# Values of the differential attention computed two heads at a time, with 512 columns moving

## The chip, the cores and the metric

One NeuronCore of one Trainium2 chip runs the program. The metric is device time in microseconds (us) of one execution. TensorE (PE) multiplies matrices, PEld is its loading of the stationary operand, VectorE (DVE) and ScalarE (ACT) work element by element, GpSimd (POOL) and SyncE (SP) here mostly issue transfers. Each engine works through its own queue of instructions in order and waits on semaphores for the others.

## The reference, cut to what matters

A decoder trunk of two layers on 512 tokens of width 1024, in float32. Layer 0 mixes tokens by pooling, layer 1 by differential attention over a shared K/V; each layer also attends to 256 memory tokens and ends in a SwiGLU. What the change touches is the product that gives the shared values, and the product that uses them:

```python
kv = rmsnorm(h, g_kv) @ w_kv
k = kv[..., :DIFF_HEADS * 2 * DIFF_HD].reshape(b, s, DIFF_HEADS, 2, DIFF_HD)
v = kv[..., DIFF_HEADS * 2 * DIFF_HD:].reshape(b, s, DIFF_HEADS, DIFF_VD)
...
sc = jnp.einsum('bqhcd,bkhcd->bhcqk', qi, k).astype(jnp.float32) * scale
p = jax.nn.softmax(sc, axis=-1)
a = p[:, :, 0] - lam * p[:, :, 1]
return jnp.einsum('bhqk,bkhe->bqhe', a.astype(v.dtype), v)
```

There are 4 heads, and a head's values are 256 columns wide.

## The kernel before, in words

Every product is made in three: each operand is split into a high part and a low rest (`split`: ScalarE writes `hi`, a rounded copy, VectorE writes `lo`, source minus `hi`), and TensorE adds hi·hi, hi·lo and lo·hi into one bank of PSUM (`three`, `group`). So each weight tile of 512 KB is loaded by a DMA on SP into `raw` (line 198), cast by ScalarE to `whi` (line 177), and subtracted by VectorE to `wlo` (line 178). The pools for `raw`, `whi` and `wlo` have three buffers each.

The weight tiles stand in one list, `plan`, in the order of use. `weights()` hands out the next tile and calls `load_to`, which writes down the transfer and the split of the tiles up to two further on (`AHEAD`). So the two tiles that come next have their splits written into the queues while the present one is multiplied.

The second layer's attention part is a list of units, `SECOND`. A letter is a kind of unit, a figure which one: `Q` and `K` queries and keys of a differential head (PSUM tiles `qk`, 48 matmuls), `V` its values (tiles `v`), `q`, `k`, `v` the same of the memory attention, `h` an output tile of the memory attention (tiles `wo`, 24 matmuls), `a` and `b` the output of the differential attention for heads 0, 1 and 2, 3. Between the pieces of these units the planner `Pace` puts the matmuls of chains that run along: for the differential attention of head n, scores of 128 queries at a time (`dsc`, two products and a bfloat16 mask for each), transposes of the probabilities (`dtr`), the product with the values (`do`, after the event `dv`), and the norm of the result (`ps_st`, `ps_row`). ScalarE makes the exponentials `dp` and the splits `ath` of the transposes, VectorE the maxima `dmx`, the differences `dp` and the rests `atl`.

`diff_values(n)` of before is a call of `token_major`: for one head, the tokens are stationary in tiles of 128, and the weights of the head move, 256 columns at a time. One PSUM bank takes two token tiles, and all 8 blocks of the contraction are done for a token tile before the next one begins. Its two weight tiles hold 4 blocks of 256 columns each. When a bank is done, `leave` reads it in two halves, each with a `split` that multiplies by the tokens' scale `rc1` (ScalarE line 180, VectorE line 181).

The PSUM pool of these tiles (`ps_mm`) has four banks. TensorE's instructions are always kept in the program's order. Those of ScalarE and VectorE may be put in another order by the scheduler that builds the program; `queued` binds a split to the program's order while `first_loads[0]` is true, which in before it is only during the first loads of the kernel.

Of the kernel before, what the change touches and what calls it, by code (L numbers as in the profile page):

```python
# [16 lines left out]
P = 128  # L17
# [4 lines left out]
KD = D // P  # L22
KF = DFF // P
NT = S // P
# [12 lines left out]
AHEAD = 2  # L37
# [20 lines left out]
       (((0, 1), "", "sync"), ((4,), "pool", "sync"), ((2, 3), "", "scalar"), ((6,), "", "scalar"), ((7,), "", "sync"),  # L58
        ((5,), "pool", "scalar")))
R_C = 6.2  # L60
SECOND = "Q0 k0 q0 k1 v0 q1* v1 Q1 k2 q2* Q2 k3 Q3 q3* v2 v3 K0 h0 h1 h2 V0 h3 h4 K1 V1 h5 K2 V2 K3 a0 a1 a2 V3 a3 h6 h7 b0 b2 b1 b3"
WARM = (256, 256, 256, 256)
FIRST = "q0 q1 k0 i0 i2 i1 o0 k1* v0 o1 v1 i3 o2 k2 q2* o3 k3 v2 q3* v3"
PARTS = 2
# [41 lines left out]
def trunk(ctx, tc, xT, memT, w_in, w_out, w_out1, w_gate, w_up, w_down, w_mk, w_mv, pool_w, w_k, w_v,  # L106
          gains, lams, c_ident, c_mask, c_rope, c_cnt, out):
    nc = tc.nc
    V, A = nc.vector, nc.scalar
    pace = Pace()  # L110
    first_loads = [True]
# [11 lines left out]
    def slot(name, shape=(2, S), dtype=F32R, parts=P):  # L123

        return slots.tile([parts, *shape], dtype, tag="s", name=name)
# [7 lines left out]
    def duo(name):  # L133

        t = slot(name)
        return t[:, 0, :], t[:, 1, :]
# [4 lines left out]
    def mmps(name="mm"):  # L141
        return ps_mm.tile([P, S], F32, tag="mm", name=name)
# [10 lines left out]
    def mm(ps, l, r, start, stop, **more):  # L153
        tc.keep_in_program_order(nc.tensor.matmul(ps, lhsT=l, rhs=r, start=start, stop=stop, **more))  # L154
# [4 lines left out]
    def group(ps, terms, first=True, last=True, **more):  # L159
        n = len(terms)  # L160
        for i, (l, r) in enumerate(terms):
            mm(ps, l, r, first and i == 0, last and i == n - 1, **more)
            if i % 6 == 5 or i == n - 1:
                yield "pe", (i % 6 + 1) * r.shape[-1] / 2370

    def three(whi, wlo, xhi, xlo):
        return [(whi, xhi), (whi, xlo), (wlo, xhi)]

    def queued(ins):

        if first_loads[0]:
            tc.keep_in_program_order(ins)

    def split(src, hi, lo, scale=None):

        if scale is None:
            queued(A.copy(out=hi, in_=src))  # L177
            queued(V.tensor_tensor(out=lo, in0=src, in1=f(hi), op=ALU.subtract))  # L178
        else:
            queued(A.activation(out=hi, in_=src, func=AF.Copy, scale=scale))  # L180
            queued(V.scalar_tensor_tensor(out=lo, in0=src, scalar=scale, in1=f(hi), op0=ALU.mult, op1=ALU.subtract))


    class Load:
# [7 lines left out]
        def tiles(self):  # L192
            self.raw = raw_tile(self.kt, self.cols)
            self.hi, self.lo = cut_tiles(self.kt, self.cols)

        def part(self, ks):
            raw, hi, lo = [t[:, ks, :] for t in (self.raw, self.hi, self.lo)]
            nc.sync.dma_start(out=raw, in_=self.src[:, ks, :])
            split(raw, hi, lo)

        def fetch(self):
# [7 lines left out]
    plan, loaded, used, fetched = [], [], [0], [0]  # L209

    def load_to(n):
        while len(loaded) < min(n, len(plan)):
            i = len(loaded)
            while fetched[0] < len(plan) and fetched[0] <= i + plan[fetched[0]].early:
                plan[fetched[0]].fetch()
                fetched[0] += 1
            loaded.append(plan[i].parts())

    def weights():

        used[0] += 1
        load_to(used[0] + (AHEAD if isinstance(plan[min(used[0], len(plan) - 1)], Load) else AHEAD7))
        return loaded[used[0] - 1]

    def unit(loads, go, need=None):
        plan.extend(x if hasattr(x, "parts") else Load(*x) for x in loads)
        return go, need
# [14 lines left out]
    h = [res.tile([P, S], F32, tag=f"h{k}", name=f"h{k}") for k in range(KD)]  # L242
# [165 lines left out]
    def tile_of(src, kt=KD):  # L408
        return [(src[:, ks:min(ks + KD, kt), :], min(KD, kt - ks), P) for ks in range(0, kt, KD)]

    def proj(ps, xs, kt=KD):

        for ks in range(0, kt, KD):
            n = min(KD, kt - ks)
            whi, wlo = weights()
            terms = []
            for k in range(n):
                terms += three(whi[:, k, :], wlo[:, k, :], xs[0][ks + k], xs[1][ks + k])
            yield from group(ps, terms, ks == 0, ks + n == kt)
# [5 lines left out]
    mo = {0: [], 1: []}  # L425
# [32 lines left out]
    def token_major(src, xs, nt, cols, store, event, after):  # L458


        def go():
            w = [weights() for _ in range(2)]
            x, out = xs(), []
            for t2 in range(nt // 2):
                ps = mmps("v")
                a, b = duo("v")
                for m in range(2):
                    t = 2 * t2 + m
                    tk = slice(t * P, (t + 1) * P)
                    o = slice(m * 256, (m + 1) * 256)  # L470
                    terms = []
                    for k in range(KD):
                        whi, wlo = w[k // 4]
                        terms += three(x[0][k][:, tk], x[1][k][:, tk], whi[:, k % 4, :], wlo[:, k % 4, :])
                    yield from group(ps[:, o], terms)
                out.append((a, b))
                yield "spawn", leave(ps, t2, out)

        def leave(ps, t2, out):
            yield "need", after  # L480
            a, b = out[t2]
            for m in range(2):
                t = 2 * t2 + m
                o = slice(m * 256, (m + 1) * 256)
                split(ps[:, o], a[:, o], b[:, o], cols[:, t:t + 1])
            if t2 == nt // 2 - 1:
                store[event[1:]] = out
                pace.at(event, 2.0)

        return unit([(src[c], 4, 256) for c in range(2)], go)  # L490
# [83 lines left out]
    def out_tile(src, j, tiles, need=None, after=None):  # L574


        def go():
            t = tiles()
            ps = mmps("wo")
            yield from proj(ps, ([a for a, _ in t], [b for _, b in t]))  # L580
            V.tensor_tensor(out=h[j], in0=ps, in1=h[j], op=ALU.add)
            if after is not None:
                after(j)

        return unit(tile_of(src[j]), go, need)

    def out_pair(src, jj, tiles, need=None, after=None):


        def go():  # L590
            t = tiles()
            whi, wlo = weights()
            for i in range(2):
                j = 2 * jj + i
                ps = mmps("wo")
                sl = slice(i * P, (i + 1) * P)
                terms = []
                for k in range(4):
                    terms += three(whi[:, k, sl], wlo[:, k, sl], *t[k])
                yield from group(ps, terms)  # L600
                V.tensor_tensor(out=h[j], in0=ps, in1=h[j], op=ALU.add)
                if after is not None:
                    after(j)

        return unit([(src[jj], 4, 256)], go, need)
# [255 lines left out]
    diff_q, diff_k, diff_v = {}, {}, {}  # L861
# [30 lines left out]
    def diff_qk(src, n, xs, store, event, rb=None, need=None):  # L892
        def go():
            pss = []
            for c in range(2):
                ps = mmps("qk")
                yield from proj(ps, xs())
                pss.append(ps)
            store[n] = roped(pss, rb)
            pace.at((event, n), R_ROPE)  # L900

        return unit(tile_of(src[2 * n]) + tile_of(src[2 * n + 1]), go, need)

    def diff_values(n):
        return token_major(w_v[n], lambda: xk, NT, rc1, diff_v, ("dv", n), "rb1")

    def diff_scores(n, probs, s0):
        yield "need", ("dk", n)
# [88 lines left out]
    norm0, norm1, xk = Norm(G_MIX), Norm(G_MIX + 8), ([], [])  # L997
# [13 lines left out]
    for step in FIRST.split():  # L1011
        n = int(step[1])
# [6 lines left out]
    rc1 = const.tile([P, NT], F32, name="rc1")  # L1019
    rb1 = slot("rb1", (S,), F32)  # L1020

    def resplit():
        yield "need", ("dq", 3)
        for k in range(KD):
# [5 lines left out]
    kinds = {"q": lambda n, need: mem_queries(1, n, x1, need), "k": lambda n, need: mem_keys(1, n, need),  # L1030
             "v": lambda n, need: mem_values(1, n), "Q": lambda n, need: diff_qk(w_in[1], n, x1, diff_q, "dq"),
             "K": lambda n, need: diff_qk(w_k, n, lambda: xk, diff_k, "dk", rb1, ("ds", n - 1) if n else "xk"),
             "V": lambda n, need: diff_values(n), "h": lambda n, need: out_tile(w_out[2], n, lambda: mo[1], ("mo", 1, 3)),
             "a": lambda n, need: out_pair(w_out1[0], n, lambda: mix1[:4], ("mix", 1)),
             "b": lambda n, need: out_pair(w_out1[1], n, lambda: mix1[4:], ("mix", 3), norm_f[1])}
    for step in SECOND.split():
        n = int(step[1])
# [5 lines left out]
    def after(j):  # L1043
        for i in range(2):
            hj = h[j][:, i * NM:(i + 1) * NM]
            half[i].add(hj)
            if j < KD - 1:
                A.activation(out=hj, in_=hj, func=AF.Copy, scale=gain(G_FINAL, j))
        if j == 2:
            A.activation(out=small(2, "warm"), in_=half[0].acc[:, :2], func=AF.Sqrt)  # L1050
# [233 lines left out]
```

## Time and profile before

| | |
|---|---|
| median of 3 runs | 1344.39 us (1343.96 to 1345.23) |
| the profiled execution | 1344.07 us |
| its span, first to last instruction | 1342.3 us |
| busy: PE, DVE, ACT, POOL | 99%, 63%, 49%, 8% |
| TensorE's granted clock, mean | 0.998 |

How to read it: a busy share is the time in which at least one instruction of the engine was running. Matmuls overlap, one starts while the one before still drains, so the duration of a matmul is longer than the time it takes from the stream; what it takes is the distance from its start to the next start. A row of the timeline merges neighbours of one kind (x2, x3), and shows in brackets how long the engine stood idle before it and which instruction of which engine ended that.

### The profile page before, as it was taken

Reading aid. Unit: us, or ns where it says so; the run is one execution under the profiler, and the core shown is the slowest. Engines: PE = TensorE matmul, PEld = TensorE weight load, DVE = VectorE, ACT = ScalarE, POOL = GpSimd, SP = SyncE. Lnnn points to the kernel's source line nnn. Section 1 sums busy time; section 2 is a strip of 40 time slices with the busy share of each in tenths; the row PEclk is TensorE's granted clock in tenths of the full one; section 3 lists DMA queues with packets and bytes.
Section 4 is the critical chain, followed back from the end, with each engine's and each line's share of the span. In section 5 each row is a group of like instructions: output and inputs, shape, how many; then the busy total and the mean of one; then the engine's idle time right before and its main releaser. Section 6 shows DMA issues by size and latency. Waiting matters only on the chain.

```text
span 1342.3 us, 17977 instructions
## 1 busy us (share of the span) xinstructions
PE 1329.8 (99%) x6948; PEld 1138.1 (85%) x6948; DVE 841.6 (63%) x1382; ACT 658.3 (49%) x1092; POOL 104.5 (8%) x86
## 2 busy tenths in 40 slices
PE   9999999999999999999999999999999999999997
PEld 7898988888888898888988988888878888898887
DVE  8887543875566693337555865688596656586332
ACT  7354532555555572225444633454465555565321
POOL 0000000023222100000000000000012222300000
PEclk9999999999999999999999999999999999999999
DMA  6333333599998823234333322222369999833321
GB/s 238 105 118 115 113 95 94 125 220 163 181 192 173 170 68 102 86 106 149 111 110 95 110 79 79 79 63 63 104 146 194 175 198 184 158 98 101 112 86 63
DMA packets 109126, 168.59 MB, mean 126 GB/s; under 512 B 5936, under 2 KB 84528, under 8 KB 109040
## 3 DMA queue, kind: packets, MB, share of 16 engines
q1 hardware_dynamic: 65680, 124.54, 29.8%
q0 software_dynamic: 42240, 41.95, 20.7%
q8 instruction: 54, 0.88, 0.3%
q10 hardware_dynamic: 1120, 0.96, 0.2%
q14 instruction: 32, 0.26, 0.1%
HBM read 165.33 MB, written 2.10 MB: 125 GB/s over the span
## 4 chain that ended last, share of the span: by engine, by line
PE 97%; DMA 1%; DVE 1%; ACT 0%; issue 0%; SPq 0%; DVEq 0%; POOLq 0%; ACTq 0%
PE down L154 18%; PE ffr L154 18%; PE wo L154 13%; PE ffq L154 8%; PE v L154 7%; PE qk L154 7%; PE mq L154 6%; PE ffz L154 4%; PE mk L154 3%; PE z L154 3%; PE msc L154 2%; PE mo L154 2%; PE htr L157 1%; PE dsc L154 1%; PE do L154 1%; PE py L154 1%
## 5 line engine op out<-in xcount | busy, mean ns | idle before, releaser
L178 DVE TENSOR_TENSOR wlo<-raw,whi 128x1024 fp32r<-128x1024 f32 (+2 forms) x226 | 267.7, 1185 | 221.1 <-ACT whi L177 217.7
L177 ACT CAST whi<-raw 128x1024 fp32r<-128x1024 f32 (+2 forms) x226 | 230.8, 1021 | 357.2 <-PE down L154 119.1
L154 PE MATMUL down<-hidp,whi 128*128 128x512 f32 (+1 forms) x748 | 220.0, 378 | 0.0
L178 DVE TENSOR_TENSOR wlo<-rawa,whi 128x1024 fp32r<-128x1024 f32 (+1 forms) x108 | 116.8, 1083 | 75.7 <-ACT whi L177 60.5
L154 PEld LDWEIGHTS down<-hidp,whi 128*128 128x128 f32 x748 | 137.3, 188 | 25.8
L177 ACT CAST whi<-rawa 128x1024 fp32r<-128x1024 f32 (+1 forms) x108 | 101.5, 941 | 103.3 <-PE ffr L154 43.9
L154 PE MATMUL down<-hidp,wlo 128*128 128x512 f32 (+1 forms) x374 | 140.9, 377 | 0.0
L637 POOL DMA_DIRECT2D rawa<-in_w_up x40 | 51.5, 1286 | 997.9 <-ACT sq L263 530.8
L154 PE MATMUL ffr<-whi,xa 128*128 128x512 f32 (+1 forms) x384 | 110.3, 372 | 0.7 <-ACT c L723 0.7
L154 PEld LDWEIGHTS ffr<-whi,xa 128*128 128x128 f32 x384 | 70.1, 188 | 13.7 <-ACT c L723 1.1
L154 PEld LDWEIGHTS down<-hidp,wlo 128*128 128x128 f32 x374 | 70.3, 188 | 12.7
L154 PE MATMUL mq<-x,whi 128*128 128x512 f32 x256 | 79.6, 392 | 0.7 <-ACT whi L177 0.6
L154 PE MATMUL qk<-x,whi 128*128 128x512 f32 x256 | 80.0, 394 | 0.0
L154 PE MATMUL wo<-mo,whi 128*128 128x512 f32 x256 | 79.5, 392 | 0.0
L154 PE MATMUL ffr<-wlo,xa 128*128 128x512 f32 (+1 forms) x192 | 71.4, 372 | 0.0
L154 PEld LDWEIGHTS mq<-x,whi 128*128 128x128 f32 x256 | 47.6, 188 | 11.4 <-ACT whi L177 1.4
L154 PE MATMUL ffr<-whi,xb 128*128 128x512 f32 (+1 forms) x192 | 56.1, 376 | 0.0
L154 PE MATMUL ffz<-whi,xb 128*128 128x512 f32 (+1 forms) x192 | 56.0, 376 | 0.0
L154 PEld LDWEIGHTS wo<-mo,whi 128*128 128x128 f32 x256 | 47.4, 188 | 9.5
L154 PE MATMUL ffq<-whi,xc 128*128 128x512 f32 (+1 forms) x192 | 55.2, 372 | 0.0
L154 PE MATMUL ffq<-whi,xe 128*128 128x512 f32 (+1 forms) x192 | 55.2, 371 | 0.0
L154 PE MATMUL ffr<-whi,xc 128*128 128x512 f32 (+1 forms) x192 | 55.1, 371 | 0.0
(241 smaller groups left out, 2742.5 us busy)
## 6 DMA issues: line engine op xcount, KB each, us to landing
rawa<-in_w_up POOLq DMA_DIRECT2D x40, 512.0 KB, 6.0
raw<-in_w_down SPq DMA_DIRECT2D x34, 512.0 KB, 3.6
raw<-in_w_out SPq DMA_DIRECT2D x32, 512.0 KB, 3.6
raw<-in_w_in SPq DMA_DIRECT2D x30, 512.0 KB, 3.6
raw<-in_w_gate SPq DMA_DIRECT2D x20, 512.0 KB, 5.4
rawa<-in_w_gate SPq DMA_DIRECT2D x20, 512.0 KB, 6.6
raw<-in_w_up SPq DMA_DIRECT2D x20, 512.0 KB, 5.9
raw<-in_w_up POOLq DMA_DIRECT2D x20, 512.0 KB, 6.1
```

The costliest lines, as they stand in the source:

```text
L154: tc.keep_in_program_order(nc.tensor.matmul(ps, lhsT=l, rhs=r, start=start, stop=stop, **more))
L157: tc.keep_in_program_order(nc.tensor.transpose(out=out, in_=in_, identity=ident))
L177: queued(A.copy(out=hi, in_=src))
L178: queued(V.tensor_tensor(out=lo, in0=src, in1=f(hi), op=ALU.subtract))
L637: nc.gpsimd.dma_start(out=t, in_=src, accum_op=ALU.add)
```

## The change

`diff_values(b)` is now written out for two heads, as the unit `W`. Four PSUM banks are taken, one for each token tile of 128. The contraction goes in four passes of two blocks each; in a pass every token tile is stationary in turn, and the weights of both heads move, 512 columns at a time. A weight tile holds two blocks of the contraction for both heads, still 512 KB, fetched by a transfer with one more dimension (`part`). After the last pass each bank is read in two halves, one for each head, with the same splits as before.

Units are put in another order: two `W` take the place of the four `V`, the first right after `K0`, the second between `K2` and `K3`, and the `h` and `a` units are spread differently.

`weights(False)` hands out a tile without writing down the ones further on. The last two passes of a `W` use it, so the tiles of the next unit are written down late, when the third token tile of the last pass is reached; `first_loads` is true from the end of the first token tile of the last pass until that is written, so that the splits of the first two token tiles and those of the next two weight tiles keep the program's order.

```diff
-SECOND = "Q0 k0 q0 k1 v0 q1* v1 Q1 k2 q2* Q2 k3 Q3 q3* v2 v3 K0 h0 h1 h2 V0 h3 h4 K1 V1 h5 K2 V2 K3 a0 a1 a2 V3 a3 h6 h7 b0 b2 b1 b3"
+SECOND = "Q0 k0 q0 k1 v0 q1* v1 Q1 k2 q2* Q2 k3 Q3 q3* v2 v3 K0 W0 h0 K1 h1 h2 h3 K2 W1 K3 h4 h5 a0 a2 a1 h6 a3 h7 b0 b2 b1 b3"
...
-            nc.sync.dma_start(out=raw, in_=self.src[:, ks, :])
+            if len(self.src.shape) == 3:
+                nc.sync.dma_start(out=raw, in_=self.src[:, ks, :])
+            else:
+
+                raw, hi, lo = raw.rearrange("p n (k c) -> p n k c", k=2), *[t.rearrange("p k (n c) -> p n k c", n=2) for t in (hi, lo)]
+                nc.sync.dma_start(out=raw, in_=self.src)
             split(raw, hi, lo)
...
-    def weights():
+    def weights(ahead=True):
 
         used[0] += 1
+        if not ahead:
+            load_to(used[0])
+            return loaded[used[0] - 1]
         load_to(used[0] + (AHEAD if isinstance(plan[min(used[0], len(plan) - 1)], Load) else AHEAD7))
         return loaded[used[0] - 1]
...
-    def diff_values(n):
-        return token_major(w_v[n], lambda: xk, NT, rc1, diff_v, ("dv", n), "rb1")
+    def diff_values(b):
+
+
+        def go():
+            pss = [mmps("v") for _ in range(NT)]
+            heads = [[duo("v") for _ in range(NT // 2)] for _ in range(2)]
+            for i in range(KD // 2):
+
+                whi, wlo = weights(i < KD // 2 - 2)
+                for t, ps in enumerate(pss):
+                    tk, terms = slice(t * P, (t + 1) * P), []
+                    if i == KD // 2 - 1 and t == 2:
+                        load_to(used[0] + AHEAD)
+                        first_loads[0] = False
+                    for k in range(2):
+                        xh, xl = xk[0][2 * i + k], xk[1][2 * i + k]
+                        terms += three(xh[:, tk], xl[:, tk], whi[:, k, :], wlo[:, k, :])
+                    yield from group(ps, terms, i == 0, i == KD // 2 - 1)
+                    if i == KD // 2 - 1:
+
+                        first_loads[0] = t < 2
+                        for n, v in enumerate(heads):
+                            o = slice(t % 2 * 256, (t % 2 + 1) * 256)
+                            split(ps[:, n * 256:(n + 1) * 256], *[x[:, o] for x in v[t // 2]], rc1[:, t:t + 1])
+            for n, v in enumerate(heads):
+                diff_v[2 * b + n,] = v
+                pace.at(("dv", 2 * b + n), 3.0)
```

How the instructions stand in the queues, with the numbers of the buffers. **First place, before:** ScalarE from the middle of `V0` to its end. `whi_7009` are the weights of the unit that follows `V0` (`wo_7196`), `whi_7015` those of the one after that; `v_7020` is the first bank of `V0`.

```order
L177 CAST whi_7009<-raw_7008 128x1024
L177 CAST ath_6936<-dtr_7057 128x2x128
L926 ACTIVATE dp_7043,s0_5267<-dsc_7036,dmx_7034,pos1_5263 128x384
L926 ACTIVATE dp_7052,s1_7035<-dsc_7045,dmx_7034,pos1_5263 128x384
L180 ACTIVATE v_7021<-v_7020,rc1_133 128x256
L177 CAST ath_6936<-dtr_7121 128x2x128
L926 ACTIVATE dp_7107,s0_5267<-dsc_7100,dmx_7098,pos1_5263 128x512
L180 ACTIVATE v_7021<-v_7020,rc1_133 128x256
L926 ACTIVATE dp_7116,s1_7099<-dsc_7109,dmx_7098,pos1_5263 128x512
L177 CAST ath_6937<-dtr_7121 128x128
L177 CAST whi_7015<-raw_7014 128x1024
```

The weights of the next unit stand ahead of everything that belongs to the last scores inside `V0`.

**First place, after:** TensorE at the end of `W0`: the last matmul of the fourth token tile (bank `v_6859`), the scores of the fourth block of queries, three transposes, and the next unit, `h0` (`wo_7115` with the weights `whi_7053`, `wlo_7054`).

```order
L154 MATMUL v_6859<-whi_6895,x_6738 128x512
L154 MATMUL dsc_7082<-r_6849,r_5363 128x512 x3
L154 LDWEIGHTS ident_b_99
L154 MATMUL dsc_7082<-mask_b_148,ident_b_99 128x128
L154 MATMUL dsc_7091<-r_6853,r_5367 128x512 x3
L154 LDWEIGHTS ident_b_99
L154 MATMUL dsc_7091<-mask_b_148,ident_b_99 128x128
L157 MATMUL dtr_7103<-ident_98,dp_7019 128x128 x3
L154 MATMUL wo_7115<-mo_5740,whi_7053 128x512 x2
L154 MATMUL wo_7115<-mo_5740,wlo_7054 128x512
```

And ScalarE there; `v_6856`, `v_6857` and `v_6858` are the banks of the first three token tiles.

```order
L962 ACTIVATE dp_7028,s1_7011<-dsc_7021,dmx_7010,pos1_5263 128x384
L180 ACTIVATE v_6860<-v_6856,rc1_133 128x256
L177 CAST ath_6941<-dtr_7103 128x2x128
L180 ACTIVATE v_6862<-v_6856,rc1_133 128x256
L180 ACTIVATE v_6860<-v_6857,rc1_133 128x256
L180 ACTIVATE v_6861<-v_6858,rc1_133 128x256
L962 ACTIVATE dp_7089,s0_5267<-dsc_7082,dmx_7080,pos1_5263 128x512
L180 ACTIVATE v_6862<-v_6857,rc1_133 128x256
L177 CAST whi_7053<-raw_7052 128x1024
L177 CAST whi_7059<-raw_7058 128x1024
```

The cast of the next unit's weights now stands six instructions behind the split `ath_6941`, which reads the three transposes.

**Second place, before:** ScalarE where the weights of `K3` are cast (`whi_7770`, for `qk_8016`), which is ahead of `V2`, the unit before `K3`.

```order
L926 ACTIVATE dp_7697,s1_7680<-dsc_7690,dmx_7679,pos1_5263 128x512
L177 CAST ath_7540<-dtr_7702 128x128
L177 CAST whi_7770<-raw_7769 128x1024
L177 CAST ath_7539<-dtr_7741 128x2x128
L878 COPY rg_7754<-r32_7750 32x512
```

**Second place, after:** ScalarE at the end of `W1`, with the banks `v_7609` to `v_7612` of its four token tiles; `whi_7908` are the weights of `K3` (`qk_7939`), the unit that follows `W1`'s last matmul on TensorE with nothing between them.

```order
L177 CAST ath_7729<-dtr_7885 128x128
L180 ACTIVATE v_7613<-v_7609,rc1_133 128x256
L180 ACTIVATE v_7615<-v_7609,rc1_133 128x256
L180 ACTIVATE v_7613<-v_7610,rc1_133 128x256
L180 ACTIVATE v_7614<-v_7611,rc1_133 128x256
L180 ACTIVATE v_7614<-v_7612,rc1_133 128x256
L180 ACTIVATE v_7615<-v_7610,rc1_133 128x256
L177 CAST whi_7908<-raw_7907 128x1024
L177 CAST whi_7914<-raw_7913 128x1024
```

The cast of `K3`'s weights moved behind a read of the fourth token tile's bank, `v_7612`, which is `W1`'s last.

## Rows read from the trace of the kernel before

**Rows 1.** The page's first part: busy us, share of the span, instructions.
```profile
PE 1329.8 (99%) x6948; PEld 1138.1 (85%) x6948; DVE 841.6 (63%) x1382; ACT 658.3 (49%) x1092; POOL 104.5 (8%) x86
```

**Rows 2.** Groups by line and form, PE: count, busy us, mean ns, idle before.
```profile
L154 PE MATMUL v<-whi,x 128*128 128x256 f32 x256 | 48.8, 286 | 0.0
L154 PE MATMUL v<-wlo,x 128*128 128x256 f32 x128 | 36.2, 283 | 0.0
```

**Rows 3.** Timeline, PE: start us, us, instruction; 12 rounds of `wo`, 10 of `v`.
```profile
778.68 0.62 PE L154 MATMUL wo<-mo,whi 128*128 128x512 f32 x2
...
786.84 0.62 PE L154 MATMUL wo<-mo,whi 128*128 128x512 f32 x2
...
799.52 0.40 PE L154 MATMUL v<-whi,x 128*128 128x256 f32 x2
...
803.11 0.40 PE L154 MATMUL v<-whi,x 128*128 128x256 f32 x2
```

**Rows 4.** Timeline, PE: the last scores of head 0, inside `V0`.
```profile
803.59 0.86 PE L154 MATMUL dsc<-r 128*128 128x512 f32 x3
...
805.18 0.50 PE L157 MATMUL dtr<-ident,dp 128*128 128x128 f32 x3
805.44 0.36 PE L154 MATMUL v<-whi,x 128*128 128x256 f32 x1
805.64 0.28 PE L154 MATMUL v<-wlo,x 128*128 128x256 f32 x1
```

**Rows 5.** Timeline, ACT, from the same scores on.
```profile
804.49 0.47 ACT L180 ACTIVATE v<-v,rc 128x256 fp32r<-128x256 f32 x1 [3.15 <-PE dsc L154]
805.72 0.37 ACT L177 CAST ath<-dtr 128x256 fp32r<-128x256 f32 x1 [0.76 <-PE dtr L157]
805.99 0.79 ACT L926 ACTIVATE dp<-dsc,dmx,pos 128x512 f32<-128x512 f32 x1
...
806.75 0.47 ACT L180 ACTIVATE v<-v,rc 128x256 fp32r<-128x256 f32 x1
807.11 0.79 ACT L926 ACTIVATE dp<-dsc,dmx,pos 128x512 f32<-128x512 f32 x1
...
807.86 0.28 ACT L177 CAST ath<-dtr 128x128 fp32r<-128x128 f32 x1
...
811.90 0.48 ACT L180 ACTIVATE v<-v,rc 128x256 fp32r<-128x256 f32 x1 [0.34 <-PE v L154]
812.27 1.04 ACT L177 CAST whi<-raw 128x1024 fp32r<-128x1024 f32 x1
```

**Rows 6.** Timeline, DVE, the same stretch.
```profile
808.63 0.75 DVE L932 SCALAR_TENSOR_TENSOR dp<-dp,s 128x512 f32<-128x512 f32 x1
...
812.62 0.47 DVE L181 SCALAR_TENSOR_TENSOR v<-v,rc 128x256 fp32r<-128x256 f32 x1
813.34 1.22 DVE L178 TENSOR_TENSOR wlo<-raw,whi 128x1024 fp32r<-128x1024 f32 x1 [0.25 <-ACT whi L177]
```

**Rows 7.** Timeline, PE: four places where TensorE waited, idle us and releaser.
```profile
866.16 0.55 PE L157 MATMUL dtr<-ident,dp 128*128 128x128 f32 x3 [0.16 <-DVE atl L178]
...
906.67 0.63 PE L157 MATMUL dtr<-ident,dp 128*128 128x128 f32 x4 [0.17 <-DVE dp L932]
...
1005.59 0.50 PE L154 MATMUL ffq<-wlo,xe 128*128 128x512 f32 x1 [0.87 <-DVE wlo L178]
1017.00 0.73 PE L154 MATMUL ffr<-whi,xa 128*128 128x512 f32 x2 [0.70 <-ACT c L723]
```

**Rows 8.** Windows: PE, PEld, DVE, ACT, POOL busy us (instructions), granted clock, DMA share, GB/s.
```profile
796.00:812.00 16.00, 16.00 (x126) 14.92 (x125) 9.87 (x24) 7.27 (x17) 0.00 (x0) 1.00 0.12 34
1000.00:1020.00 20.00, 18.43 (x80) 14.60 (x79) 17.79 (x39) 10.82 (x17) 6.46 (x5) 1.00 1.07 173
1336.00:1343.00 7.00, 0.00 (x0) 0.00 (x0) 1.68 (x5) 0.14 (x1) 1.41 (x2) 0.50 0.44 151
```

**Rows 9.** DMA issues: KB each, median us from issue to landing.
```profile
raw<-in_w_v SPq DMA_DIRECT2D x8, 512.0 KB, 3.6
```

More of the change, by code (lines that the diff above doesn't have):

```diff
@@ L902, in diff_qk @@
         return unit(tile_of(src[2 * n]) + tile_of(src[2 * n + 1]), go, need)
-    def diff_values(n):
-        return token_major(w_v[n], lambda: xk, NT, rc1, diff_v, ("dv", n), "rb1")
+    def diff_values(b):
[21 more added lines that the diff above has]
+                pace.at(("dv", 2 * b + n), 3.0)
+        return unit([(w_v[2 * b:2 * b + 2, i // 2, :, 2 * (i % 2):2 * (i % 2) + 2, :].rearrange("n p k c -> p n k c"), 2, 512)
+                     for i in range(KD // 2)], go)
     def diff_scores(n, probs, s0):
@@ L1032, in trunk @@
              "K": lambda n, need: diff_qk(w_k, n, lambda: xk, diff_k, "dk", rb1, ("ds", n - 1) if n else "xk"),
-             "V": lambda n, need: diff_values(n), "h": lambda n, need: out_tile(w_out[2], n, lambda: mo[1], ("mo", 1, 3)),
+             "W": lambda n, need: diff_values(n), "h": lambda n, need: out_tile(w_out[2], n, lambda: mo[1], ("mo", 1, 3)),
              "a": lambda n, need: out_pair(w_out1[0], n, lambda: mix1[:4], ("mix", 1)),
```

## The prediction

> **What bounds the kernel now.** The first part of the page comes first: TensorE is busy for 1329.8 of the span's 1342.3 us, and no other engine is above 63% [rows 1]. So a change is worth what it takes from or adds to TensorE's stream; work of the other engines counts only where TensorE has to wait for it. The windows say the same of the stretch that is changed: 16.00 of 16.00 us busy at a granted clock of 1.00 between 796 and 812 us, with VectorE at 9.87 and ScalarE at 7.27 [rows 8]. Next the timeline of TensorE, in which the brackets name the waits. Between 770 and 1020 us there are four of weight: two before transposes of `dtr`, 0.16 and 0.17 us, and two at the start of the second feed-forward part, 0.87 and 0.70 us [rows 7]. Everywhere else in this part TensorE passes from one unit to the next without a gap, because the weights of the next unit were split well ahead: the order before has the cast of the following unit's weights (`whi_7009`) ahead of the last scores and of every read of `V0`'s banks. Last the timelines of ScalarE and VectorE around the end of such a unit, since the change puts other work there [rows 5, 6].
>
> **The change part by part: columns.** A matmul's price is the distance between starts. Twelve rounds of three `wo` matmuls with 512 columns take 786.84 - 778.68 = 8.16 us, 0.2267 us each; ten rounds of three `v` matmuls with 256 columns take 803.11 - 799.52 = 3.59 us, 0.1197 us each [rows 3]. There are 256 + 128 = 384 `v` matmuls [rows 2], and 192 of twice the width after: 384 x 0.1197 = 45.96 against 192 x 0.2267 = 43.52, a gain of 2.44 us, all of it on the path. The small matmuls that break into the stream (scores, transposes, norm) are the same in number, and TensorE's order has 70 returns from transposes or scores to wide products before and after; each costs the first wide matmul some 0.08 us more than its pace (805.64 - 805.44 = 0.20 against 0.12 [rows 3, 4]), so they cancel. I keep 2.1 to 2.7 as bounds.
>
> **First weights of the unit after `W0`.** This is a wait that before has nowhere, so it is worked out from the queues. ScalarE's order after has, in front of `whi_7053`, the split `ath_6941` of the transposes `dtr_7103`, then four reads of `v` banks and an exponential. Those transposes are TensorE's last work ahead of `h0`. Count from the start of the last scores, t = 0. Before has the same scores, 512 columns wide and followed by three transposes, at 803.59: the transposes start at t = 1.59, the next wide product at 1.85 [rows 4], and the split `ath` starts at 805.72, which is 2.13, ended by the transposes [rows 5]. From there ScalarE's instructions follow at distances that rows 5 show: `ath` to the next 0.27 (805.72 to 805.99), a read of `v` 0.36 (806.75 to 807.11), the exponential with the reading of its sum 0.76 (805.99 to 806.75). So the cast `whi_7053` starts at 2.13 + 0.27 + 3 x 0.36 + 0.76 + 0.36 = 4.60 and, at 1.04, ends at 5.64. TensorE would have begun `h0` at 1.85. Two matmuls then run with `whi`, and the third needs `wlo_7054`, 1.22 us on VectorE directly behind the cast as the row of before has it (813.34 behind 812.27 + 1.04 [rows 5, 6]): 5.67 + 1.22 = 6.89, against 1.85 + 0.08 + 2 x 0.2267 = 2.38. The loss is 4.5 us. If the third matmul finds `wlo` ready it is 3.8; if each of ScalarE's instructions takes its whole duration instead of the distance (0.37, 4 x 0.47, 0.79, then 1.04 and 1.22) it is 5.1.
>
> **First weights of the unit after `W1`.** Here `K3` follows `W1`'s last matmul at once, and `whi_7908` stands behind a read of that very matmul's bank. Count from the slot in which `K3` should begin. The last matmul still drains some 0.16 us into it (two take 0.62, the pace is 0.2267 [rows 3]), and ScalarE starts a few hundredths later, as at 811.90 [rows 5]: 0.20. Then one more read, and the cast: 0.20 + 0.36 + 0.36 + 1.04 = 1.96, `wlo` at 1.99 + 1.22 = 3.21, where the third matmul was due at 0.45: 2.8 us lost. ScalarE reaches that read in time: the last exponential and split of the scores are over 807.86 + 0.28 - 803.59 = 4.55 after the scores began, while the scores, the transposes and three token tiles of `W1` take 1.85 + 0.08 + 18 x 0.2267 = 6.0, and four reads at 0.36 fill the difference exactly. That is tight, and the second half of a bank is read only after VectorE's rest of the first half, which stands behind a `dp` of 0.75 [rows 6]; so up to 3.5. The lower bound is 2.0, with `wlo` in time.
>
> **What the other moves cost.** The beginnings of `W0` and `W1` cost nothing: their first tiles are still split two ahead, under the 48 matmuls of a `K`. The transfers are as many and as large; each reads shorter runs, and lands 3.6 us after its issue before [rows 9]. SP issues it when its buffer is free, two tiles of 24 x 0.2267 = 5.4 us ahead, so even twice 3.6 is covered; without that cover it would be up to 3.6 a tile. POOL has nothing queued there [rows 8]. The product `do` of head 1 falls into the first pass of `W1` and takes the two banks that `W1` still needs; the third token tile waits for ScalarE's copy of the first half, which the twelve matmuls of the second half cover: 0, at most a read of 0.47. Of the two waits for transposes [rows 7] the order has one place of the same kind left, so I count 0.17 us saved, 0 to 0.33. The last units, `b0 b2 b1 b3`, are unchanged, and so are the waits of 0.87 and 0.70 behind them.
>
> **Sum.** -2.44 - 0.17 + 4.5 + 2.8 = +4.7 us on the profiled execution's 1344.07 us (0.32 below the median): 1348.8, and 1349.1 for a median like the one shown. With the bounds: -2.7 - 0.33 + 3.8 + 2.0 = +2.8, and -2.1 + 0.5 + 5.1 + 3.5 = +7.0; 1347.2 to 1351.4.
>
> **Rivals.** (1) Not slower: the binding works, and the casts are done in time. Place: the two ends of `W`; it decides at 2.6 us, the sum of the gains. For it: the weights have landed long before, the cast is only 1.04 us, and ScalarE is busy for less than half of this stretch [rows 8]; if it reached `whi` straight behind the first read, only pieces of the 1.22 us for `wlo` would be left. Against it: the two orders, in which the casts stand behind instructions that TensorE itself releases late, and ScalarE's rows of before, which keep the listed order to the letter [rows 5]. With no wait 1344.39 - 2.6 = 1341.8; with half a `wlo` or so at each end 1343 to 1344; with half of my waits 1345.4. 18%.
>
> (2) The clock falls in the wait after `W0`. TensorE idles there for about 3.6 us; the longest idle in this part of before is 0.87 us, and in the windows the clock stays at 1.00, the level of 2.4 GHz, through those [rows 7, 8]. It is at 0.50, the level of 1.2 GHz, only in the last 7 us, where no matmul runs [rows 8]. If it fell here, `h0`'s matmuls would take twice as long until it rose: at most 24 x 0.2267 = 5.4 us for the whole unit, half of that for half; 1351.8 with the half. 6%. The Trainium skill speaks against the change here ("TensorE: Matmul & The Clock Gate", HAM oscillation): idle stretches between bursts of matmuls are what brings the lower clock back; no row of before has a mid-kernel stretch as long, so the trace leaves it open.
>
> (3) The columns cost the same in either form, so the change does not make TensorE's own work shorter: no gain, 1349.1 + 2.4 = 1351.5. Rows 3 speak against it, unless weights as moving operand behave otherwise at 512 than activations do. 4%. The Trainium skill's spacing of warm matmuls ("TensorE: Matmul & The Clock Gate", Back-to-back issue gap) is N/2.4 + 2.5 ns, 109.2 and 215.8 ns; by it the gain would be an estimated 0.5 us and the time about 1351. The rows have 119.7 and 226.7 ns, and they decide.
>
> **How the numbers follow.** My forecast has 72%: 1349.1, itself between 1347.2 and 1351.4. A measurement of this kernel tells about 0.2% from no change, 2.7 us: slower is above 1347.1, faster below 1341.7. Slower is the forecast with rivals 2 and 3, 82%; rival 1 is mostly within the bound, 12%, and 6% faster. The range 1346.0 to 1351.8 leaves out most of rival 1 and the upper half of rival 2.
>
> **What the profile after would show.** `v` with 512 columns, 192 of them at a pace of 0.227 us. An idle of PE before the first `wo` after `W0`, ended by ACT `whi`, of 3 to 4 us, and a shorter one two matmuls later ended by DVE `wlo`; the same pair before the `qk` after `W1`, near 2 and 0.8 us. On ACT, `ath` ended by PE `dtr`, and then `whi` some 2.5 us behind it. The granted clock at 1.00 throughout. I am wrong if TensorE passes from `W0` to `h0` without a gap, or if the gaps are there and later waits disappear in their place.

## The result, and the profile after

The changed kernel takes 1352.14 us (median, 1351.34 to 1352.62) beside 1344.36 of the kernel before on the same chip: a ratio of 1.0056, 95% interval 1.0043 to 1.0069. The profiled execution takes 1351.91 us, 7.84 more than the one before. The forecast was 1349.1 and its range ended at 1351.8: slower, as forecast, but by more than the range allowed.

The page's first part, as [rows 1], shows TensorE still busy for 99%, and 2.3 us longer, though it has 192 matmuls less:

```profile
PE 1332.1 (99%) x6756; PEld 1130.5 (84%) x6756; DVE 843.2 (62%) x1382; ACT 657.6 (49%) x1092; POOL 104.5 (8%) x86
```

The groups by line and form answer to [rows 2] (count, busy us, mean ns of one, idle before): 192 matmuls of 512 columns in the place of 384 of 256.

```profile
L154 PE MATMUL v<-whi,x 128*128 128x512 f32 x128 | 42.0, 397 | 0.0
...
L154 PE MATMUL v<-wlo,x 128*128 128x512 f32 x64 | 24.9, 390 | 0.0
```

The timeline of TensorE at the end of `W0`, against [rows 4] (start us, us, instruction; in brackets the idle time before it and what ended it):

```profile
803.79 0.84 PE L154 MATMUL dsc<-r 128*128 128x512 f32 x3
...
805.37 0.50 PE L157 MATMUL dtr<-ident,dp 128*128 128x128 f32 x3
809.49 1.22 PE L154 MATMUL wo<-mo,whi 128*128 128x512 f32 x2 [3.63 <-ACT whi L177]
810.75 0.80 PE L154 MATMUL wo<-mo,wlo 128*128 128x512 f32 x1
...
813.18 0.39 PE L154 MATMUL wo<-mo,wlo 128*128 128x512 f32 x1
```

`h0`'s first matmul starts 5.70 us after the scores, the third 6.96; without a wait the third was due at 2.38. ScalarE and VectorE at the same place, against [rows 5] and [rows 6]:

```profile
805.90 0.37 ACT L177 CAST ath<-dtr 128x256 fp32r<-128x256 f32 x1 [0.76 <-PE dtr L157]
806.17 1.21 ACT L180 ACTIVATE v<-v,rc 128x256 fp32r<-128x256 f32 x3
807.25 0.80 ACT L962 ACTIVATE dp<-dsc,dmx,pos 128x512 f32<-128x512 f32 x1
...
808.01 0.50 ACT L180 ACTIVATE v<-v,rc 128x256 fp32r<-128x256 f32 x1
808.37 1.07 ACT L177 CAST whi<-raw 128x1024 fp32r<-128x1024 f32 x1
```

```profile
809.47 2.36 DVE L178 TENSOR_TENSOR wlo<-raw,whi 128x1024 fp32r<-128x1024 f32 x2 [0.45 <-ACT whi L177]
```

The weights that `h0` waits for are cast behind one split, four reads of banks and an exponential, all of them after the transposes; the rest `wlo` (the first of the two) follows the cast at once. The same pair of waits stands at the end of `W1`, ahead of `K3`:

```profile
898.33 0.39 PE L154 MATMUL v<-whi,x 128*128 128x512 f32 x1
900.74 0.73 PE L154 MATMUL qk<-x,whi 128*128 128x512 f32 x2 [2.02 <-ACT whi L177]
902.00 0.79 PE L154 MATMUL qk<-x,wlo 128*128 128x512 f32 x1 [0.53 <-DVE wlo L178]
...
905.31 0.40 PE L154 MATMUL qk<-x,wlo 128*128 128x512 f32 x1
```

ScalarE's last five reads of banks ahead of that cast, which follows them at once, at 899.64:

```profile
897.82 1.94 ACT L180 ACTIVATE v<-v,rc 128x256 fp32r<-128x256 f32 x5 [0.55 <-DVE v L181]
```

What the forecast's sum did not count stands in the windows (start and end, length, busy us of PE, PEld, DVE, ACT, POOL with instructions, then the granted clock, DMA share, GB/s), against [rows 8]:

```profile
805.90:809.40 3.50, 0.00 (x0) 0.00 (x0) 2.81 (x8) 3.50 (x9) 0.00 (x0) 1.00 0.00 0
809.42:812.83 3.41, 3.30 (x7) 2.19 (x8) 3.36 (x7) 3.41 (x8) 0.00 (x0) 0.50 0.29 83
812.83:820.00 7.17, 7.17 (x35) 5.93 (x35) 4.72 (x8) 2.33 (x5) 0.00 (x0) 1.00 0.50 182
898.00:901.50 3.50, 1.45 (x6) 0.56 (x4) 3.19 (x7) 3.50 (x7) 0.00 (x0) 1.00 0.00 0
901.58:904.99 3.41, 2.99 (x9) 2.50 (x10) 3.41 (x5) 1.76 (x5) 0.00 (x0) 0.50 0.52 155
904.99:912.00 7.01, 7.01 (x39) 6.18 (x39) 0.86 (x3) 2.28 (x5) 0.00 (x0) 1.00 0.42 149
```

Behind each of the two waits the granted clock is 0.50, the level of 1.2 GHz, for 3.41 us: 7 matmuls in the first of these stretches and 9 in the second, small ones included (a part of each stretch is still wait), where 3.41 us hold 15 of 512 columns at a pace of 0.2267. The first fall coincides with TensorE's return to work, the second comes 0.8 us after it.

### The profile page after: what moved, and what is told of

Its sections match the earlier page's. It is cut to its first block, busy times and chain, and to the rows that moved or that the text cites. A ratio compares the mean times of both kernels' runs of the same rounds, so it can differ in the third digit from the quotient of the medians.

```text
span 1350.0 us, 17581 instructions
## 1 busy us (share of the span) xinstructions
PE 1332.1 (99%) x6756; PEld 1130.5 (84%) x6756; DVE 843.2 (62%) x1382; ACT 657.6 (49%) x1092; POOL 104.5 (8%) x86
## 4 chain that ended last, share of the span: by engine, by line
PE 96%; ACT 1%; DVE 1%; DMA 1%; issue 0%; SPq 0%; DVEq 0%; POOLq 0%; ACTq 0%
PE down L154 18%; PE ffr L154 17%; PE wo L154 13%; PE ffq L154 8%; PE qk L154 7%; PE mq L154 6%; PE v L154 6%; PE ffz L154 4%; PE mk L154 3%; PE z L154 3%; PE msc L154 2%; PE mo L154 2%; PE htr L157 1%; PE dsc L154 1%; PE do L154 1%; PE py L154 1%
## 5 line engine op out<-in xcount | busy, mean ns | idle before, releaser
L154 PEld LDWEIGHTS qk<-x,whi 128*128 128x128 f32 x256 | 47.3, 190 | 11.3 <-ACT whi L177 2.4
```

## Experiments

Theory after the result: (A) the two waits are the forecast ones, caused by the casts standing behind the reads; (B) on top of them the lower clock costs time in both places. Rivals: that the waits are the whole loss and the clock is only a symptom; that the order of units, the wide products or the binding cost something by themselves.

**The clock: TensorE kept running in the waits.**

```diff
             for n, v in enumerate(heads):
                 diff_v[2 * b + n,] = v
                 pace.at(("dv", 2 * b + n), 3.0)
+            dead = trps("fill")
+            for _ in range((15, 8)[b]):
+                mm(dead, xk[0][KD - 1][:, :P], whi[:, 1, :], True, True)
```

> The changed kernel, with 15 matmuls of 512 columns put behind W0's last scores and transposes and 8 behind W1's last matmul; nobody reads their product. They fill 15 x 0.2267 = 3.4 and 8 x 0.2267 = 1.8 us of the two idle times of TensorE (3.63 and 2.02 us) and leave the late weights as they are. Theory (the clock fell because TensorE stood idle, and that cost is apart from the waits): the first matmuls of h0 and K3 start as late as before, the granted clock stays at 1.00 in both places, and the 2 x 3.41 us at 0.50, in which each matmul takes twice its time, give back 2 x 1.7 = 3.4 us: 1352.1 - 3.4 = 1348.7. Rival (the waits are the whole loss, or the clock falls for another reason than the idle time): about 1352.1, with the clock at 0.50 in both places as now. If only the first place is idle long enough to matter: 1350.4.

Measured 1350.77 us (1350.07 to 1350.88, four runs), ratio 1.0044 [1.0029, 1.0059], 2.1 above the expected 1348.7. This interval overlaps that of the changed kernel, which ran beside other runs of before; so both were run once more on one chip.

> The changed kernel itself, beside the next one on the same chip. Theory (both waits as before, and the clock falls behind both in most executions): 1352.1, and a mean granted clock of 0.996 in most executions. If the falls come only in part of the executions, as behind the shorter waits of the kernels with the order of units swapped, the times lie in steps between 1349.8 and 1352.1, and the lower ones go with the higher mean clock.

> The kernel with matmuls in the two idle times, whose product nobody reads, once more beside the changed kernel. In the traces the third matmuls of h0 and K3 come equally late in both, and from there to a fixed later matmul the changed kernel takes 0.93 us longer at the first place (5.83 against 4.90) and 1.37 at the second (5.37 against 4.00). Theory (this is the price of the lower clock, and all that the filling changes): 2.3 us below the changed kernel, 1349.8, at a mean granted clock of 0.998. Rival (the filling is no cause, the first pair of runs differed by the start of the program): the same time as the changed kernel within 0.5 us.

Measured side by side: the changed kernel 1353.43 us (1352.59 to 1355.49, five runs), ratio 1.0068 [1.0055, 1.0081]; with the filling 1350.41 us (1349.89 to 1350.61, five runs), ratio 1.0041 [1.0027, 1.0055]. No run of one overlaps the other. Both medians lie above what was expected, 1352.1 and 1349.8, and they differ by 3.0 where 2.3 was expected. The mean granted clock is 0.993 to 0.996 in the runs of the changed kernel and 0.997 to 0.998 with the filling. The timeline of TensorE with the filling, first place and then second:

```profile
805.73 3.68 PE L154 MATMUL fill<-whi,x 128*128 128x512 f32 x15
809.61 0.73 PE L154 MATMUL wo<-mo,whi 128*128 128x512 f32 x2 [0.19 <-ACT whi L177]
810.87 0.50 PE L154 MATMUL wo<-mo,wlo 128*128 128x512 f32 x1 [0.53 <-DVE wlo L178]
811.20 0.63 PE L154 MATMUL wo<-mo,whi 128*128 128x512 f32 x2
...
812.36 0.39 PE L154 MATMUL wo<-mo,wlo 128*128 128x512 f32 x1
...
901.15 0.50 PE L154 MATMUL qk<-x,wlo 128*128 128x512 f32 x1 [0.53 <-DVE wlo L178]
...
903.09 0.40 PE L154 MATMUL qk<-x,wlo 128*128 128x512 f32 x1
```

and its window behind the first place:

```profile
809.60:813.00 3.40, 2.87 (x11) 2.10 (x12) 3.40 (x7) 3.40 (x7) 0.00 (x0) 1.00 0.24 66
```

The weights are as late as before, the clock stays up. From the third matmul to the ninth it is 812.36 - 810.87 = 1.49 us here and 813.18 - 810.75 = 2.43 in the first profile of the changed kernel: 0.94 for the clock. At the second place it is 1.94 against 3.31: 1.37. Together 2.3 us, where I had expected 3.4 at first: part of the low stretch lies in the wait for `wlo`, where it costs nothing. In its second profile the changed kernel paid more, because the clock stayed low for twice as long at the first place:

```profile
807.60:814.60 7.00, 5.79 (x13) 4.11 (x14) 6.30 (x13) 5.13 (x10) 0.00 (x0) 0.51 0.44 145
```

So (B) holds: 2.3 us in the first profile, 3.0 between the medians of the pair. The rival falls. The filling does not touch (A): 1350.41 is still 6 us above before.

**The waits: ordinary look-ahead.** The last two passes of `W` ask for their weights as all other units do, and nothing is bound.

```diff
-                whi, wlo = weights(i < KD // 2 - 2)
+                whi, wlo = weights()
...
-                    if i == KD // 2 - 1 and t == 2:
-                        load_to(used[0] + AHEAD)
-                        first_loads[0] = False
...
-                        first_loads[0] = t < 2
```

> The changed kernel with the ordinary look-ahead of two tiles in W, and without the binding of the splits; order of the units and 512 columns as changed. Theory (the weights written down late are the cause of both waits): no wait for weights at h0 and at K3, none at all at K3. At h0 a smaller wait is left for its PSUM bank, the one of W0's first token tile: its second half is read behind the split of the last transposes on ScalarE, and VectorE's rest of it follows. In the queues, with the distances of the kernel before, that is 2.5 us. 1352.1 - 7.5 - 3.4 + 2.5 = 1343.7 to 1344.3 if the clock stays up, 1345.9 if 2.5 us of idle bring it down there once. Rival (the wide products, the transfers with one more dimension, or the order of the units cost the time): 1349 or more.

Measured 1347.19 us (1345.11 to 1347.77, ten runs), ratio 1.0017 [1.0008, 1.0027]. The waits for weights are gone at both places, and one wait of the changed part is left:

```profile
810.12 1.22 PE L154 MATMUL wo<-mo,whi 128*128 128x512 f32 x2 [2.60 <-DVE v L181]
```

VectorE's read of the first token tile's bank releases it. Behind it the clock is low again (0.58 over the 4 us from 809.50). The median is 1.3 above the expected 1345.9; in the profiled execution the clock also fell in the program's first 10 us, behind an idle time of 1.47 us there, ahead of anything that the change touches; whether that is so in most runs the times don't tell.

**Late or bound?** The late writing and the binding were then taken apart. Late, but not bound:

```diff
                     if i == KD // 2 - 1 and t == 2:
                         load_to(used[0] + AHEAD)
-                        first_loads[0] = False
...
-                        first_loads[0] = t < 2
```

> The changed kernel with its late writing of the next tiles kept, and only the binding to the program's order taken out. In the queues that the scheduler then makes, the casts of h0's and K3's weights stand ahead of the last scores again, though they are written late. Theory (late writing costs only together with the binding): no wait for weights at either place; what is left is the wait of h0's first matmul for its bank, 2.6 us as in the run with the ordinary look-ahead, and a fall of the clock behind it; 1346 to 1347, like that run. Rival (late writing costs by itself): 1350 or more, with TensorE waiting for whi and wlo at h0 and K3.

Measured 1345.60 us (1344.26 to 1347.43, ten runs), ratio 1.0008 [0.9998, 1.0017]: 0.4 below the expected range, and in the profiled execution the clock did not fall. Bound, with the ordinary look-ahead:

```diff
-                whi, wlo = weights(i < KD // 2 - 2)
+                whi, wlo = weights()
...
-                    if i == KD // 2 - 1 and t == 2:
-                        load_to(used[0] + AHEAD)
-                        first_loads[0] = False
```

> The other half: ordinary look-ahead, and the splits of the first two token tiles bound to the program's order. Theory (the binding by itself costs nothing, since the casts are already ahead of the bound reads): no wait for weights; at h0 a wait for the bank of some 2.1 us (0.4 less than unbound, because the bank's second read comes earlier), perhaps 0.3 at K3 for its bank; with one fall of the clock 1345.5 to 1346.5. Rival (the binding by itself holds up the queues): 1349 or more.

Measured 1346.17 us (1344.54 to 1347.93, ten runs), ratio 1.0011 [1.0002, 1.0021].

Late but not bound, ScalarE's cast of `h0`'s weights and TensorE's start of `h0`:

```profile
804.07 1.05 ACT L177 CAST whi<-raw 128x1024 fp32r<-128x1024 f32 x1 [2.20 <-issue]
```

```profile
808.50 0.73 PE L154 MATMUL wo<-mo,whi 128*128 128x512 f32 x2 [2.60 <-DVE v L181]
```

The cast now begins 0.24 us after the last scores have begun (803.83), not 4.58 after them. Bound but written early, the same wait is shorter by 0.4, as expected, and `K3` waits 0.26 us for its bank:

```profile
807.97 0.73 PE L154 MATMUL wo<-mo,whi 128*128 128x512 f32 x2 [2.21 <-DVE v L181]
```

Neither half brings a wait for weights at these two places; each leaves the kernel near 1346, and only both together give 1352 and more. Here the scheduler puts a cast that was written late back into its place, as long as nothing binds it; and the binding does no harm to the casts that were written early. So the step to blame is the pair.

**The scores ahead of the cast.** The changed kernel, late and bound, with one unit moved:

```diff
-... K0 W0 h0 K1 h1 h2 h3 K2 W1 K3 ...
+... K0 h0 W0 K1 h1 h2 h3 K2 W1 K3 ...
```

> The changed kernel, late and bound, with only h0 put ahead of W0, so that the last scores of head 0 lie 5.4 us ahead of W0's end. Theory (what made the first wait longer than the second is that the transposes and exponentials of the last scores stand ahead of the cast on ScalarE; without them the cast waits for the bank reads alone): at W0's end, now ahead of K1, 0.3 to 2.0 us for whi and 0.8 for wlo, at W1's end 2.0 and 0.5 with the clock at 0.50 as before. Against the version without any wait (1342.6) that is 1.1 to 3.0, and 3.0 + 1.4 for the second place, and 0 to 1.4 for a fall of the clock in the first: 1348.1 to 1351.4. Rival (the scores are not the reason): as the changed kernel, 1352.

Measured 1347.23 us (1345.24 to 1348.98, ten runs), ratio 1.0020 [1.0011, 1.0029]: 0.9 below the expected range. TensorE at the ends of `W0` and `W1`, and the window behind the second:

```profile
811.47 0.73 PE L154 MATMUL qk<-x,whi 128*128 128x512 f32 x2 [0.20 <-ACT whi L177]
812.73 0.50 PE L154 MATMUL qk<-x,wlo 128*128 128x512 f32 x1 [0.53 <-DVE wlo L178]
...
895.86 0.73 PE L154 MATMUL qk<-x,whi 128*128 128x512 f32 x2 [2.01 <-ACT whi L177]
897.12 0.50 PE L154 MATMUL qk<-x,wlo 128*128 128x512 f32 x1 [0.53 <-DVE wlo L178]
```

```profile
897.00:901.00 4.00, 3.88 (x19) 3.25 (x20) 3.56 (x7) 2.18 (x5) 0.00 (x0) 1.00 0.62 179
```

The wait of 3.63 us at `W0` has shrunk to 0.20, so the last scores, whose transposes hold up ScalarE's queue, were the reason that the first place was the worse one. The pair at `W1` is as before. But the clock did not fall behind it this time, though the idle times are the same to 0.01 us. That is 1.4 of the 1.7 us by which the profiled execution (1346.41) stays below the expected range; the rest is that the two waits at `W0` are 0.73 us together, where at least 1.1 was expected. In how many of the ten runs the clock fell, the times don't tell.

**The order of units alone.** Two units of before stand in the place of each `W`:

```diff
+        parts = [token_major(w_v[n], lambda: xk, NT, rc1, diff_v, ("dv", n), "rb1") for n in (2 * b, 2 * b + 1)]
...
         def go():
-            pss = [mmps("v") for _ in range(NT)]
...
+            for g, _ in parts:
+                yield from g()
```

> The order of units as changed, but in the place of each W two V units of before (256 columns moving, ordinary look-ahead, nothing bound). Theory (the order by itself costs nothing, all of it is in how W handles its end): 1344.4, no wait of TensorE over 0.4 us between 770 and 1000 us. Rival (the units spread differently bring waits of their own, which the changed kernel would then have too): 1346 or more, with the waits at h1 to h7, a0 to a3 or the transposes.

Measured 1344.32 us (1343.70 to 1345.98, ten runs), ratio 0.9999 [0.9989, 1.0009]. The order costs nothing measurable; its longest wait between 770 and 1000 us is one for transposes:

```profile
806.68 0.55 PE L157 MATMUL dtr<-ident,dp 128*128 128x128 f32 x3 [0.16 <-DVE atl L178]
```

**The columns alone.** The ordinary look-ahead, nothing bound, and `h0` ahead of `W0`, which also gives the banks time to be read:

```diff
-... K0 W0 h0 K1 h1 h2 h3 K2 W1 K3 ...
+... K0 h0 W0 K1 h1 h2 h3 K2 W1 K3 ...
...
-                whi, wlo = weights(i < KD // 2 - 2)
+                whi, wlo = weights()
...
-                    if i == KD // 2 - 1 and t == 2:
-                        load_to(used[0] + AHEAD)
-                        first_loads[0] = False
...
-                        first_loads[0] = t < 2
```

> W with 512 columns, ordinary look-ahead and nothing bound, and h0 ahead of W0 instead of behind it, so that W0 ends some 5.4 us after the last scores of head 0, as W1 ends after head 1's. Theory (late weights and, without them, a bank read behind the last scores are all that W costs; the columns gain 2.4 us): no wait at either end of W, 1344.4 - 2.44 - 0.17 = 1341.7. Rival (512 columns do not gain in this place, or something else in W costs): 1344 or more.

Measured 1342.56 us (1340.96 to 1344.34, ten runs), ratio 0.9984 [0.9974, 0.9993]: a little faster than before too, by 2.0 us where 2.6 were expected. The list of TensorE's waits between 770 and 1030 us (total us, times, longest) has nothing left of `W`, and at its end `K3` follows without a gap:

```profile
PE ffq L154 <- DVE wlo L178: 0.9, 1, 0.9
PE dtr L157 <- DVE atl L178: 0.2, 1, 0.2
PE ffr L154 <- ACT c L731: 0.2, 1, 0.2
```

```profile
892.66 0.39 PE L154 MATMUL v<-whi,x 128*128 128x512 f32 x1
892.89 0.62 PE L154 MATMUL qk<-x,whi 128*128 128x512 f32 x2
```

Whole executions also differ outside the changed part, so this part is best measured by itself: from the first matmul behind `K0` to the first of the feed-forward part that follows (`ffr`). The pairs are of before, of the changed kernel, of the one with the filling (second time), and of this one:

```profile
778.00 0.62 PE L154 MATMUL wo<-mo,whi 128*128 128x512 f32 x2
...
987.29 0.62 PE L154 MATMUL ffr<-whi,xa 128*128 128x512 f32 x2
...
778.45 0.39 PE L154 MATMUL v<-whi,x 128*128 128x512 f32 x1
...
995.35 0.61 PE L154 MATMUL ffr<-whi,xa 128*128 128x512 f32 x2
...
778.56 0.39 PE L154 MATMUL v<-whi,x 128*128 128x512 f32 x1
...
993.13 0.62 PE L154 MATMUL ffr<-whi,xa 128*128 128x512 f32 x2
...
778.44 0.61 PE L154 MATMUL wo<-mo,whi 128*128 128x512 f32 x2
...
985.20 0.61 PE L154 MATMUL ffr<-whi,xa 128*128 128x512 f32 x2
```

These are 209.29, 216.90, 214.57 and 206.76 us. With no waits at the ends, the wide products gain 2.5 us on before. Against this kernel the one with the filling loses 7.8 us, which is the price of the two waits, and the changed kernel 2.3 more, which is the price of the clock (3.7 in its second profile, from 777.73 to 996.02). The order alone takes 209.36, from 778.30 to 987.66, the same as before, and has no wait that moving `h0` could have removed; moving `h0` by itself was not run.

## Why the prediction was right, and where it failed

**Columns: right.** -2.44 us forecast. The pace of the wide `v` matmuls is that of the `wo` matmuls in [rows 3] (`K3` follows the last one after 892.89 - 892.66 = 0.23), and the kernel without waits gains 2.5 us on the changed part. Rival 3 falls. By the spacing that the Trainium skill gives for an isolated matmul ("TensorE: Matmul & The Clock Gate", Back-to-back issue gap) the gain would have been an estimated 0.5 us; the trace speaks against it.

**The order of units and the transfers: right at nothing.** The order alone measures 0.9999. The transfers of these weights land in 3.7 us, before in 3.6 [rows 9], and TensorE waits for none. Of the two waits for transposes one is left, as counted.

**The first wait: right.** The third matmul was forecast 6.89 us after the scores began and comes at 6.96; a loss of 4.6 against 4.5. The reason given, that the transposes release what stands ahead of the cast, is shown by moving `h0` ahead: 3.63 us of waiting for `whi` become 0.20. **The second: right in size.** From the start of the last `v` matmul to the third of `K3` it is 902.00 - 898.33 = 3.67 us, where 0.68 was due: 3.0 against 2.8. But the forecast had ScalarE reach the read of the last bank just in time, and the trace has it late: the five reads run back to back from 897.82, after a wait for VectorE's rest of the first bank, so the fourth of them, by the order of the queue that of the last bank, begins at an estimated 898.9 (their 1.94 us divided evenly), while the last matmul is over at 898.33 + 0.39 = 898.72. So it is this queue of reads that sets the time of the cast, some 0.2 us behind the forecast. What the argument lacked is that neither the late writing nor the binding makes these waits alone.

**Rival 1 falls:** TensorE does wait, for whole casts. The gain that it would have kept is what the version without waits has.

**The clock: the step that failed.** The sum puts the clock at nothing, and the signs have it at 1.00 throughout. Rival 2 had 6%, one place, and half of 5.4 us. It came in both profiles of the changed kernel, at both places, and cost 0.94 + 1.37 = 2.3 us in the first of them and 3.7 in the second. I argued from a longest idle time of 0.87 us in before [rows 7, 8] that the trace left open what 3.6 us do, and then gave the open question a small chance; the second place, with 2 us of idle, I did not weigh at all. The changed part lost 7.6 us: -2.5 for the columns, 7.8 for the waits and 2.3 for the clock. These three add up by the way they were taken, but the last two also agree with the timelines: 4.6 + 3.0 for the waits, with 0.2 for the two restarts (behind the wait for `wlo` the first matmul takes 811.20 - 810.87 = 0.33 from the stream, and not 0.23), and 0.94 + 1.37 for the clock. Outside the changed part little is left of the 7.84 us: 0.45 is lost ahead of it (778.45 against 778.00), and 0.40 comes back behind it, where the forecast had nothing change: the wait of 0.70 [rows 7] is 0.30 after. The range ended at 1351.8, at the price of one fall, and so missed by 0.3. The Trainium skill's warning ("TensorE: Matmul & The Clock Gate", HAM oscillation), idle stretches between bursts of matmuls bring the lower clock back, was the page to give more weight: the runs with and without the filling agree with it.

## What to carry to other kernels

A wait that is worked out from the queues should carry a second price: behind idle times of TensorE of 2.0 to 3.6 us the following matmuls ran at half the clock in several of these runs, though not in all, and in the changed kernel that added a third to a half of what the two waits cost. Binding instructions to the program's order did harm here only where the casts were also written late; before binding reads of a bank, look at what is written behind them in the same stretch, and who waits for it. When a wider product moves all its bank reads to its end, put the unit that follows it ahead of it, so that the last scores come well before that end, rather than hold its neighbours' weights back; this gave the fastest kernel here.

## What was not expected of the hardware

The same idle time does not always have the same result. With the ordinary look-ahead TensorE stood idle for 2.60 us ahead of `h0` and the granted clock fell; late but not bound it also stood idle for 2.60 us at that place, and the clock stayed at 1.00. A wait of 2.21 us (bound, written early) was followed by the lower level. Waits of 2.02 and 0.53 us ahead of `K3` were followed by it in the changed kernel, waits of 2.01 and 0.53 at the same place with `h0` ahead were not. The windows behind two of these waits:

```profile
808.40:812.00 3.60, 3.50 (x15) 2.92 (x16) 3.48 (x13) 2.63 (x8) 0.00 (x0) 1.00 0.26 102
```

```profile
809.00:812.00 3.00, 3.00 (x8) 2.33 (x8) 2.67 (x10) 2.34 (x7) 0.00 (x0) 0.50 0.06 22
```

The first of these rows is from the kernel that is late but not bound, the second from the one that is bound and written early; they hold 15 matmuls in 3.60 us and 8 in 3.00. The Trainium skill ("TensorE: Matmul & The Clock Gate", What's actually happening) says that the activity is watched by something that runs freely and does not start with the kernel; a result that depends on when an idle time falls, and not on its length alone, agrees with that, but no run here moves one idle time against it. The times go with it: late but not bound, the fastest of ten runs (1344.26 us) has a mean granted clock of 0.998 and the slowest (1347.43) 0.995, though not every lower mean need come from this wait. A median of four runs says little about how often the clock falls.
